# One expert of a mixture-of-experts stage on quarters instead of halves of TensorE's columns, with its gather moved ahead of a branch

## Chip, cores and metric

One core of a Trainium2 chip runs the whole kernel in one launch. The metric is device time in microseconds (us) of that core, smaller is better. Engines are called as the profile calls them: PE (matrix multiply), PEld (its weight loads), DVE (vector), ACT (scalar), POOL (GpSimd) and SP (the queue that issues the large transfers). A `q` behind a name (PEldq, SPq) is the engine's sequencer, which runs branches, register loads and DMA issues.

## What is computed

Two layers of a diffusion backbone on 256 latent and 256 context tokens of width 1024. Each layer mixes tokens (attention and a gated convolution) and then channels. The first layer's channel mixer is dense; the second layer's is the part that matters here:

```
def moe_swiglu(h, w_router, w_gu, w_down):          # h: 256 x 1024
    logits = (h @ w_router).astype(jnp.float32)     # 8 experts
    top_v, top_i = lax.top_k(logits, TOP_K)         # TOP_K = 2
    top_w = jax.nn.softmax(top_v, axis=-1)
    gates = jnp.sum(jax.nn.one_hot(top_i, 8) * top_w[..., None], axis=-2)
    for e in range(8):
        g, u = jnp.split(h @ w_gu[e], 2, axis=-1)   # w_gu[e]: 1024 x 7168
        y = y + gates[..., e:e + 1] * ((silu(g) * u) @ w_down[e])   # w_down[e]: 3584 x 1024
```

Everything is float32, and each expert's weights are 42 pieces of 1 MB (28 of `w_gu`, 14 of `w_down`), read once from HBM.

## The kernel before

**Ranks.** After routing, experts are sorted by their token counts on the chip. Place 0 holds expert 0, places 1 to 7 the others, from the fullest to the emptiest. The heavy places are `HS = (0, 2, 3, 1)` and the light ones `LS = (4, 5, 6, 7)`, both in the order in which they are worked on. `keyi[p]` is eight times the count of place p plus its expert's number.

**Arms.** `tc.If(odd > 0)` holds a general path (`any_experts`) for counts that fit no plan. Its Else arm runs the plan of pairs: `plans[0]` (places 0, 2, 3 beside 4, 5 and most of 6), and then, under `tc.If(k1 > 8 * 128 + 7)`, `plans[1]` (place 1 beside the rest of 6 and all of 7) in one of two arms. `few` is the arm in which place 1 has more than 128 tokens, up to 160: its first 128 tokens run like those of every heavy expert, its last ones (at most 32) as a second small block.

**A heavy operation** (`Hg` gate, `Hu` up, `Hd` down) uses two pieces of 1 MB. Each piece is split by ACT and DVE into a high and a low part in reduced-precision format (L99, L100), and PE makes three products of them (`mm3`, L537 to L539) for 128 tokens. In the arm `few` it is followed by the last tokens' products, straight from the unsplit piece in float32, with 32 tokens on each quarter of PE's 128 columns, so four slices of the weights at a time (L1711 for gate and up, L1781 for down).

**A light operation** (`Lg`, `Lu`, `Ld`) also uses two pieces, unsplit, in float32, with 64 tokens on each half of PE's columns, so two slices of the weights at a time (L1735 gate and up, L1801 down). `Ht` and `Lt` turn the activations (L1745, L1756).

**Order.** `schedule` interleaves them: while heavy chunk s is at its gate and up, light chunk s - 1 is too, and the down products of the chunks before follow. A chunk is 1024 hidden columns, the last one 512. `plans[1]` has 48 operations that take weights, 96 pieces in all; 14 of them are `Lg` or `Lu` of place 7 and 7 are `Ld` of place 7. Inside `run_pairs` each of PE, DVE and ACT keeps the order of the program. Small jobs (gathers of an expert's tokens, `combine` of its output) stand in a queue `bg` and advance by one step after an operation; what is left is done at the end of `run_pairs`.

**Pieces.** `Mixed` issues the transfers in order on SP's queue into eight buffers (`RAW_N`). In the arm `few` a piece keeps its buffer until the last tokens' products have read it.

**The gather of the last tokens**, `few_tokens`, stands at the head of `plans[1]`: two steps on DVE build the selection (L1668, L1669), eight matmuls gather the rows (L1674), six transposes place them (L1679, L1682).

**The end.** `finish` adds the last expert's output, normalises and stores.

Of the kernel before, what the change touches and what calls it, by code (L numbers as in the profile page):

```python
# [8 lines left out]
F32 = mybir.dt.float32  # L9
# [158 lines left out]
def kernel(ctx: ExitStack, tc: tile.TileContext, x, c, cx, c_ctx, w_ada, b_ada, norm_g,  # L168
# [18 lines left out]
    def tiny(shape, name="s", dt=F32):  # L187
        return sm.tile(shape, dt, name=name, tag="sm")
# [1427 lines left out]

    X32, SL32 = {}, {}

    def light_gather(p):

        n = LS.index(p)
        tl_ = ring.tile([128, 512], F32R, "x2", 2 + n % 2)
        sl = tl_[:, 0:256].rearrange("p (t n) -> p t n", t=2)
        SL32[p] = tl_[:, 256:512]
        x32 = ring.tile([128, 512], F32, "x32", n % 2)
        X32[p] = x32.rearrange("p (k n) -> p k n", k=KD)
        for t in range(2):
            V.tensor_scalar(sl[:, t, :].rearrange("p (g n) -> p g n", g=2),
                            iota[:, 0:64].unsqueeze(1).to_broadcast([128, 2, 64]), posms[:, t, p:p + 1], None,
                            op0=OP.is_equal)  # L1630
        yield from pause(3)
        for h in range(2):
            pb, q = tbank(), slice(64 * h, 64 * h + 64)
            for i, (t, src) in enumerate(((0, hth), (0, htl), (1, hth), (1, htl))):
                PE.matmul(pb, sl[:, t, :], src[:, t, hsl(h)], start=i == 0, stop=i == 3)
            A.copy(x2f[q, :], pb[q, :])
            yield
        pb = tbank()
        for t in range(2):
            PE.transpose(pb[:, 128 * t:128 * t + 128], sl[:, t, :].bitcast(F32), ident)  # L1640
        A.copy(SL32[p], pb[:, :256])
        yield
        pb = tbank()
        for c in range(4):
            PE.transpose(pb[:, 128 * c:128 * c + 128], x2f[:, 128 * c:128 * c + 128], ident)
        A.copy(x32.rearrange("p (h c n) -> p c h n", h=2, c=4), pb.rearrange("p (c h n) -> p c h n", c=4, h=2))
        yield

    def run_pairs(plan, few, todo):

        arm[0] = "few pair" if few else "pair"
        Wb.keep = few
# [8 lines left out]
        x2, t2 = x2f[:, 0:256].rearrange("p (k n) -> p k n", k=KD), x2f[:, 256:512]  # L1661
        st2 = x2r[:, 256:512]

        def few_tokens(p):
            sl2 = x2r[:, 0:256].rearrange("p (t n) -> p t n", t=2)
            for t in range(2):
                p2 = tiny([128, 1], "p2")
                V.tensor_scalar(p2, posms[:, t, p:p + 1], -128.0, None, op0=OP.add)  # L1668
                V.tensor_scalar(sl2[:, t, :].rearrange("p (g n) -> p g n", g=4),  # L1669
                                iota[:, 0:32].unsqueeze(1).to_broadcast([128, 4, 32]), p2, None, op0=OP.is_equal)  # L1670
            for h in range(2):
                pb, q = hb[h], slice(32 * h, 32 * h + 32)
                for i, (t, src) in enumerate(((0, hth), (0, htl), (1, hth), (1, htl))):
                    PE.matmul(pb, sl2[:, t, :], src[:, t, hsl(h)], start=i == 0, stop=i == 3)  # L1674
                A.copy(fact[q, :], pb[q, :])
            yield
            pb = tr0[:, 0:256]
            for c in range(4):
                PE.transpose(pb[:, 64 * c:64 * c + 64], fact[0:64, 128 * c:128 * c + 128], ident[0:64, 0:64])  # L1679
            A.copy(x2.rearrange("p (h c) n -> p c h n", h=2), pb.rearrange("p (c h n) -> p c h n", c=4, h=2))  # L1680
            for t in range(2):
                PE.transpose(facc[:, 128 * t:128 * t + 128], sl2[:, t, :].bitcast(F32), ident)  # L1682
            A.copy(st2, facc[:, :256])
            yield

        def heavy_gu(p, c, i, up):
            x1, n = XG[p], CHUNKS[c][1]
            nb, w4, per = n // 512, n // 4, 2048 // n
            tokens = few_tokens(p) if few and c == i == 0 and not up else None
            if tokens:  # L1690
                next(tokens)
            Wb.floor = Wb.gi if few else None
            raws = []
            for t in range(2 * i, 2 * i + 2):
                wh, wl = Wb.get("mg")
                raws.append(Wb.last_raw)
                for k in range(per):
                    kk = per * t + k
                    for b in range(nb):
                        q = slice(512 * b, 512 * b + 512)  # L1700
                        mm3(hb[b], x1[:, 0, kk, :], x1[:, 1, kk, :], wh[:, k, q], wl[:, k, q], kk == 0, kk == KD - 1)
            if tokens:
                next(tokens)
            o2 = tr0[:, 256 * up:256 * up + w4]
            if few:

                for t in range(2 * i, 2 * i + 2):
                    for k in range(per):
                        kk = per * t + k
                        for g_ in range(4):  # L1710
                            PE.matmul(o2[32 * g_:32 * g_ + 32, :], x2[:, kk, :],  # L1711
                                      raws[t % 2][:, k, w4 * g_:w4 * g_ + w4], start=kk == 0, stop=kk == KD - 1)
            Wb.floor = None
            if i == nb - 1:
                evac(nb, hact, hb, up)
                if few:
                    evac(1, [fact[:, 0:w4]], [o2], up)

        def evac(nb, act, o, up):
            for b in range(nb):  # L1720
                if up:
                    V.tensor_tensor(act[b], act[b], o[b], op=OP.mult)
                else:
                    A.activation(act[b], o[b], AF.Silu)

        def light_gu(p, c, i, up):
            n = CHUNKS[c][1]
            w2, per = n // 2, 2048 // n
            o = lb[:, 0:w2]
            for t in range(2 * i, 2 * i + 2):  # L1730
                raw = Wb.get("lg")
                for k in range(per):
                    kk = per * t + k
                    for g_ in range(2):
                        PE.matmul(o[64 * g_:64 * g_ + 64, :], X32[p][:, kk, :], raw[:, k, w2 * g_:w2 * g_ + w2],  # L1735
                                  start=kk == 0, stop=kk == KD - 1)
            if i == n // 512 - 1:
                evac(1, [lact[:, 0:w2]], [o], up)

        def heavy_turn(p, c, i):  # L1740
            n = CHUNKS[c][1]
# [9 lines left out]
                A.copy(t2[:, 0:n // 4], tr0[:, 0:n // 4])  # L1751

        def light_turn(p, c, i):
            w2 = CHUNKS[c][1] // 2
            for j in range(w2 // 128):
                PE.transpose(lb[:, 128 * j:128 * j + 128], lact[:, 128 * j:128 * j + 128], ident)  # L1756
            A.copy(lt[:, 0:w2], lb[:, 0:w2])  # L1757

        def heavy_down(p, c, i):
            nb = CHUNKS[c][1] // 512  # L1760
# [30 lines left out]
                bg.append(combine(gates[:, :, p], parts, wait=1 if p == 1 else 2))  # L1791

        def light_down(p, c, i):
            nj = CHUNKS[c][1] // 256
            final = c == len(CHUNKS) - 1
            for t in range(2):
                raw = Wb.get("ld")
                for f in range(2):
                    g_, j = divmod(4 * i + 2 * t + f, nj)
                    for h in range(2):  # L1800
                        PE.matmul(lacc[64 * h:64 * h + 64, :], lt[:, 128 * j + 64 * g_:128 * j + 64 * g_ + 64],  # L1801
                                  raw[:, f, hsl(h)], start=c == 0 and i == t == f == 0, stop=final and t == 1 and f == 1)
            if final:
                o = [ring.tile([128, 512], F32R, "x2", i) for i in range(2)]
                split_hl(*o, lacc)
                S_["parts"] = [(SL32[p], in_halves(o))]
                if p != LS[-1]:
                    bg.append(combine(gates[:, :, p], S_["parts"], wait=2))

# [62 lines left out]
    for t in range(2):  # L1872
        V.scalar_tensor_tensor(gate[:, t, :], gate[:, t, :], e2[:, t:t + 1], sel[:, t, :], op0=OP.mult, op1=OP.mult)
    by_rank(gates, gate)
    odd = nc.values_load(bad[0:1, 0:1], min_val=0, max_val=NE)
    k1 = nc.values_load(keyi[0:1, 1:2], min_val=0, max_val=8 * S + 7)
    ids = [0] + [nc.values_load(eid[0:1, p:p + 1], engines=[mybir.EngineType.SP], min_val=0, max_val=NE - 1)
                 for p in range(1, NE)]
    back0 = again()
    with tc.If(odd > 0) as odd_arm:  # L1880

        Wm = Stream(nc, ring, moe_items(range(NE)))
        Wm.lag, Wm.ahead, Wm.sahead = lambda: first(-LAG["experts"]), RAW_N, SPL_N - 1
        any_experts()
# [3 lines left out]
    with odd_arm.Else():  # L1888
        run_pairs(plans[0], False, {
            ("Hg", 0, 0, 0): [lambda: light_gather(4)], ("Hg", 0, 1, 0): [lambda: gather([2, 3], posms, True)],  # L1890
            ("Hg", 0, 3, 0): [lambda: light_gather(5)], ("Hg", 2, 1, 0): [lambda: gather([1], posms, True)],
            ("Hg", 2, 3, 0): [lambda: light_gather(6)], ("Hg", 3, 2, 0): [lambda: light_gather(7)]})
        back1 = again()
        Wb.hold = len(Wb.items)
        with tc.If(k1 > 8 * 128 + 7) as few_arm:  # L1895
            finish(gates[:, :, LS[-1]], run_pairs(plans[1], True, {}))
        back1()
        with few_arm.Else():
            finish(gates[:, :, LS[-1]], run_pairs(plans[1], False, {}))
# [47 lines left out]
```

## Time and profile before

| | us |
|---|---|
| median of 3 runs | 1918.11 |
| lowest, highest | 1916.24, 1918.60 |
| profiled execution | 1916.19 |
| its span, first to last instruction | 1914.4 |
| PE busy over the span | 1818.3 |
| DVE busy, ACT busy | 948.4, 812.2 |
| bytes moved | 521.12 MB, mean 272 GB/s |

The profiled execution's time is its span and 1.8 us around it; it lies 1.9 us under the median. The stage with the experts runs from about 976 us to the end of the span. Busy PE time includes modelled ends of pipelined matmuls, so the pace of a matmul is read from the distance of two starts.

### The profile page before, as it was taken

The page shows a single profiled execution, that of the slowest core. Times are in us where ns is not written, and L with a number is a line of the kernel's source. Part 1 is how long each engine was busy: PE and PEld are TensorE (multiplying, and loading weights), DVE is VectorE, ACT ScalarE, POOL GpSimd, SP SyncE. Part 2 cuts the span into 40 slices and gives each one's busy share as a digit, 9 for nine tenths or more (in the row PEclk, how much of TensorE's full clock was granted, in tenths as well). Part 3 has the DMA queues.
Part 4 walks back from the last instruction along what each step waited for, and adds up shares of the span by engine and source line. Part 5 has one row for each costly group of instructions (what it writes and reads, how often), then busy time and mean ns, then how long its engine had stood idle before and what let it go on. Part 6 is the DMA issues. An engine that isn't in the chain of part 4 may idle for free. (4 is left out here: it accounts for less than half of the span.)

```text
span 1914.4 us, 23955 instructions
## 1 busy us (share of the span) xinstructions
PE 1818.3 (95%) x9321; PEld 1273.7 (67%) x9321; DVE 948.4 (50%) x1310; ACT 812.2 (42%) x1194; POOL 79.0 (4%) x139
## 2 busy tenths in 40 slices
PE   6999999999999999999779999999999996999997
PEld 3866679877777888877666656566565653655553
DVE  3344578322232748536556545665455543545433
ACT  3354457221212547438445535454354443434322
POOL 2200110000000000200200000000000000000001
PEclk9999999999999999999969999999999998999999
DMA  9956286645552656733438999999999998898994
GB/s 337 200 174 203 105 287 209 208 154 176 172 179 89 220 180 235 174 104 111 176 107 339 368 404 404 409 409 406 406 404 409 410 404 349 323 375 334 373 376 187
DMA packets 223760, 521.12 MB, mean 272 GB/s; under 512 B 30040, under 2 KB 83856, under 8 KB 223632
## 3 DMA queue, kind: packets, MB, share of 16 engines
q1 hardware_dynamic: 223152, 519.27, 74.3%
q8 instruction: 77, 1.26, 0.3%
q14 instruction: 51, 0.42, 0.1%
q10 hardware_dynamic: 480, 0.18, 0.0%
HBM read 518.31 MB, written 3.13 MB: 272 GB/s over the span
## 5 line engine op out<-in xcount | busy, mean ns | idle before, releaser
L100 DVE TENSOR_TENSOR wlor<-rawr,whir 128x1024 fp32r<-128x1024 f32 x336 | 395.7, 1221 | 386.3 <-ACT whir L99 375.0
L99 ACT CAST whir<-rawr 128x1024 fp32r<-128x1024 f32 x336 | 335.4, 1049 | 340.9 <-DMA rawr<-in_w_gu_moe_dram 163.1
L100 DVE TENSOR_TENSOR wlo<-raw,whi 128x1024 fp32r<-128x1024 f32 x188 | 224.6, 1222 | 113.6 <-ACT whi L99 74.5
L99 ACT CAST whi<-raw 128x1024 fp32r<-128x1024 f32 x192 | 193.0, 1049 | 143.8 <-PE pg L538 40.3
L1735 PE MATMUL gur<-rawr,x32r 128*64 128x512 f32 (+1 forms) x1024 | 205.1, 547 | 6.5 <-ACT lar L1757 5.3
L537 PE MATMUL gur<-whir,xgr 128*128 128x512 f32 x448 | 181.0, 404 | 11.8 <-issue 6.7
L538 PE MATMUL gur<-wlor,xgr 128*128 128x512 f32 x448 | 176.0, 393 | 0.0
L539 PE MATMUL gur<-whir,xgr 128*128 128x512 f32 x448 | 175.6, 392 | 0.0
L1735 PEld LDWEIGHTS gur<-rawr,x32r 128*64 128x64 f32 x1024 | 69.5, 137 | 118.2 <-issue 100.0
L537 PEld LDWEIGHTS gur<-whir,xgr 128*128 128x128 f32 x448 | 84.9, 190 | 51.1 <-issue 22.0
L1801 PE MATMUL pd<-rawr,lar 128*64 128x512 f32 x448 | 101.7, 598 | 0.5 <-ACT lar L1757 0.5
L539 PEld LDWEIGHTS gur<-whir,xgr 128*128 128x128 f32 x448 | 84.8, 189 | 18.4
L538 PEld LDWEIGHTS gur<-wlor,xgr 128*128 128x128 f32 x448 | 84.9, 189 | 16.0
L537 PE MATMUL pg<-hh,whi 128*128 128x512 f32 (+1 forms) x256 | 95.0, 372 | 0.0
L539 PE MATMUL pu<-hh,wlo 128*128 128x512 f32 (+1 forms) x256 | 93.0, 363 | 0.4 <-DVE wlo L100 0.4
L539 PE MATMUL pg<-hh,wlo 128*128 128x512 f32 (+1 forms) x256 | 93.1, 364 | 0.0
L537 PE MATMUL pu<-hh,whi 128*128 128x512 f32 (+1 forms) x256 | 92.9, 363 | 0.0
L538 PE MATMUL pg<-hl,whi 128*128 128x512 f32 (+1 forms) x256 | 92.9, 363 | 0.0
L538 PE MATMUL pu<-hl,whi 128*128 128x512 f32 (+1 forms) x256 | 92.8, 362 | 0.0
L945 DVE TENSOR_TENSOR act<-sg,pu 128x512 f32<-128x512 f32 (+1 forms) x32 | 19.8, 620 | 147.1 <-PE pu L539 128.7
L537 PE MATMUL py<-whi,ah 128*128 128x512 f32 x224 | 87.4, 390 | 0.0
L539 PE MATMUL py<-whi,al 128*128 128x512 f32 x224 | 86.8, 390 | 0.6 <-DVE al L550 0.6
(391 smaller groups left out, 2972.5 us busy)
## 6 DMA issues: line engine op xcount, KB each, us to landing
rawr<-in_w_gu_moe_dram SPq DMA_DIRECT2D x224, 1024.0 KB
rawr<-in_w_down_moe_dram SPq DMA_DIRECT2D x112, 1024.0 KB
raw<-in_w_ada_dram SPq DMA_DIRECT2D x48, 1024.0 KB
raw<-in_w_gu_dense_dram SPq DMA_DIRECT2D x32, 1024.0 KB
raw<-in_w_down_dense_dram SPq DMA_DIRECT2D x28, 1024.0 KB
raw<-in_w_in_dram SPq DMA_DIRECT2D x24, 1024.0 KB
raw<-in_w_out_dram SPq DMA_DIRECT2D x12, 1024.0 KB
BM<-rep SPq DMA_DIRECT2D x8, 512.0 KB
```

Source lines behind the costliest of these rows:

```text
L99: nc.scalar.copy(hi[:, q], flat[:, q])
L100: (nc.gpsimd if g == "G" else nc.vector).tensor_tensor(lo[:, q], flat[:, q], hi[:, q].bitcast(F32), op=OP.subtract)
L537: PE.matmul(o, wh, mh, start=first, stop=False, skip_group_check=shared)
L538: PE.matmul(o, wh, ml, start=False, stop=False, skip_group_check=shared)
L539: PE.matmul(o, wl, mh, start=False, stop=last, skip_group_check=shared)
L945: V.tensor_tensor(act[f // 4][:, f % 4, s0:s0 + n], sg, pu, op=OP.mult)
L1735: PE.matmul(o[64 * g_:64 * g_ + 64, :], X32[p][:, kk, :], raw[:, k, w2 * g_:w2 * g_ + w2], start=kk == 0, stop=kk == KD - 1)
L1801: PE.matmul(lacc[64 * h:64 * h + 64, :], lt[:, 128 * j + 64 * g_:128 * j + 64 * g_ + 64], raw[:, f, hsl(h)], start=c == 0 and i == t == f ...
```

## The change

Place 7 may run on quarters. A new condition inside the arm `few`, `tc.If(k7 < 8 * 33)`, is true if it has at most 32 tokens; then `groups(7)` is 4, and its products take 32 tokens on each quarter of PE's columns, like the last tokens' products of the heavy expert. The Else arm keeps halves. `quarter_slots` builds the selection for the way back; it and `few_gather` (the former `few_tokens`) are queued in `bg` during `plans[0]`, behind `light_gather(7)`. One more value is loaded into registers (`k7`), and the outer `If` names its false arm as the one that is to follow next in the code.

```diff
+    def quarter_slots(p):
+        sl = LQ.rearrange("p (t n) -> p t n", t=2)
+        for t in range(2):
+            V.tensor_scalar(sl[:, t, :].rearrange("p (g n) -> p g n", g=4),
+                            iota[:, 0:32].unsqueeze(1).to_broadcast([128, 4, 32]), posms[:, t, p:p + 1], None,
+                            op0=OP.is_equal)
+        yield from pause(2)
+        pb = tbank()
+        for t in range(2):
+            PE.transpose(pb[:, 128 * t:128 * t + 128], sl[:, t, :].bitcast(F32), ident)
+        A.copy(LQ, pb[:, :256])
+        yield
...
+    def few_gather(p):
...
+        yield from pause(2)
+        for h in range(2):
+            pb, q = tbank(), slice(32 * h, 32 * h + 32)
+            for i, (t, src) in enumerate(((0, hth), (0, htl), (1, hth), (1, htl))):
+                PE.matmul(pb, sl2[:, t, :], src[:, t, hsl(h)], start=i == 0, stop=i == 3)
+            A.copy(fact[q, :], pb[q, :])
+            yield
...
-            tokens = few_tokens(p) if few and c == i == 0 and not up else None
-            if tokens:
-                next(tokens)
...
+        def groups(p):
+
+            return 4 if quarters and p == LS[-1] else 2
...
-                    for g_ in range(2):
-                        PE.matmul(o[64 * g_:64 * g_ + 64, :], X32[p][:, kk, :], raw[:, k, w2 * g_:w2 * g_ + w2],
+                    for g_ in range(G):
+                        PE.matmul(o[m * g_:m * g_ + m, :], X32[p][:, kk, 0:m], raw[:, k, wg * g_:wg * g_ + wg],
                                   start=kk == 0, stop=kk == KD - 1)
...
-            w2 = CHUNKS[c][1] // 2
-            for j in range(w2 // 128):
+            wg = CHUNKS[c][1] // groups(p)
+            for j in range(wg // 128):
...
+                        q = 64 * h + 32 * f if G == 4 else 64 * h
+                        PE.matmul(lacc[q:q + m, :], lt[:, 128 * j + m * g_:128 * j + m * g_ + m], raw[:, f, hsl(h)],
...
+    k7 = nc.values_load(keyi[0:1, 7:8], min_val=0, max_val=8 * S + 7)
...
-    with tc.If(odd > 0) as odd_arm:
+    with tc.If(odd > 0, preferred_fallthrough_block=False) as odd_arm:
...
-            ("Hg", 2, 3, 0): [lambda: light_gather(6)], ("Hg", 3, 2, 0): [lambda: light_gather(7)]})
+            ("Hg", 2, 3, 0): [lambda: light_gather(6)], ("Hg", 3, 2, 0): [lambda: light_gather(7), lambda: quarter_slots(7), lambda: few_gather(1)]})
...
-            finish(gates[:, :, LS[-1]], run_pairs(plans[1], True, {}))
+            with tc.If(k7 < 8 * 33) as quarter_arm:
+                finish(gates[:, :, LS[-1]], run_pairs(plans[1], True, {}, True))
+            back1()
+            with quarter_arm.Else():
+                finish(gates[:, :, LS[-1]], run_pairs(plans[1], True, {}))
```

## Rows read from the trace of the kernel before

**Rows 1.** Windows of two stretches: busy us of each engine, PE clock, DMA share, GB/s

```profile
1100.00:1590.00 490.00, 474.88 (x2176) 292.28 (x2174) 258.92 (x258) 221.05 (x262) 0.00 (x0) 0.99 1.03 406
1640.00:1880.00 240.00, 237.48 (x1519) 138.82 (x1518) 112.31 (x112) 92.58 (x111) 0.00 (x0) 1.00 0.95 368
```

**Rows 2.** Waits of SP's queue, 1500 us to the end: total, times, longest

```profile
SPq L80 <- PE tr L1711: 112.9, 26, 22.3
```

**Rows 3.** Timeline of PE: start, us, line, operation, count [idle before]

```profile
1682.15 1.93 PE L1711 MATMUL tr<-rawr,x2f 128*32 128x256 f32 x32
1684.02 3.65 PE L1735 MATMUL gur<-rawr,x32r 128*64 128x512 f32 x16
1687.60 0.50 PE L537 MATMUL gur<-whir,xgr 128*128 128x512 f32 x1
...
1693.27 1.93 PE L1711 MATMUL tr<-rawr,x2f 128*32 128x256 f32 x32
...
1726.61 1.92 PE L1781 MATMUL pd<-rawr,x2f 128*32 128x512 f32 x16
1728.46 0.73 PE L1363 MATMUL tr<-oer,str 128*128 128x512 f32 x2
1729.12 3.65 PE L1801 MATMUL pd<-rawr,lar 128*64 128x512 f32 x16
1732.71 0.74 PE L1363 MATMUL tr<-oer,str 128*128 128x512 f32 x2
```

**Rows 4.** Windows behind the first and the second branch, columns as in Rows 1

```profile
983.00:990.00 7.00, 7.00 (x21) 5.47 (x20) 2.21 (x2) 2.37 (x3) 0.00 (x0) 0.60 0.01 4
...
1620.00:1624.00 4.00, 3.91 (x10) 3.18 (x11) 0.38 (x3) 0.78 (x2) 0.00 (x0) 0.56 0.27 109
1624.00:1630.00 6.00, 6.00 (x29) 4.39 (x28) 0.00 (x0) 0.45 (x2) 0.00 (x0) 1.00 0.00 0
```

**Rows 5.** Timeline of all engines around the second branch

```profile
1605.69 1.99 ACT L99 CAST whir<-rawr 128x1024 fp32r<-128x1024 f32 x2 [5.91 <-DMA rawr<-in_w_gu_moe_dram]
...
1607.20 0.66 PE L1756 MATMUL gur<-kc,sgr 128*128 128x128 f32 x4
...
1616.21 1.99 ACT L99 CAST whir<-rawr 128x1024 fp32r<-128x1024 f32 x2 [5.51 <-DMA rawr<-in_w_gu_moe_dram]
...
1619.57 0.15 DVE L1668 TENSOR_SCALAR p<-posms 128x1 f32<-128x1 f32 x1
...
1620.09 0.80 PE L1674 MATMUL gur<-hth,x2r 128*128 128x512 f32 x1 [12.24 <-DVE p L1668]
...
1623.60 0.40 PE L537 MATMUL gur<-whir,xgr 128*128 128x512 f32 x1
...
1629.43 0.46 PE L1679 MATMUL tr<-kc,sgr 64*128 64x64 f32 x4
...
1630.35 1.93 PE L1711 MATMUL tr<-rawr,x2f 128*32 128x256 f32 x32
```

**Rows 6.** Lines with branches, at three places: duration ns, start us

```profile
L1880 PEldq COMPARE_BRANCH  x1: 6329/6329/6329, 976.0 to 976.0; - x1
...
L1895 PEldq COMPARE_BRANCH  x1: 82/82/82, 1603.6 to 1603.6; - x1
...
L1895 PEldq COMPARE_BRANCH  x1: 3678/3678/3678, 1901.6 to 1901.6; - x1
```

**Rows 7.** PE at the first branch, and the load of one register there

```profile
982.42 0.79 PE L537 MATMUL gur<-whir,xgr 128*128 128x512 f32 x1 [6.71 <-issue]
...
L1876 PEldq TENSOR_LOAD <-keyi x1: 312/312/312, 975.6 to 975.6; - x1
```

**Rows 8.** The end of `plans[1]` on PE, and POOL's last store wait

```profile
1894.90 3.65 PE L1801 MATMUL pd<-rawr,lar 128*64 128x512 f32 x16 [0.46 <-ACT lar L1757]
1898.48 0.73 PE L1363 MATMUL tr<-oer,str 128*128 128x512 f32 x2
...
1912.50 0.09 POOL L1309 MEMSET actr<- 1x1 f32 x1 [0.63 <-DMA out_dram<-actr]
```

More of the change, by code (lines that the diff above doesn't have):

```diff
@@ L1617 @@
     X32, SL32 = {}, {}
+    LQ = ring.tile([128, 512], F32R, "x2", 3)[:, 0:256]
+    def quarter_slots(p):
[10 more added lines that the diff above has]
+        yield
     def light_gather(p):
@@ L1647, in light_gather, with run_pairs @@
         yield
-    def run_pairs(plan, few, todo):
+    def few_gather(p):
+        sl2 = x2r[:, 0:256].rearrange("p (t n) -> p t n", t=2)
+        fact = ring.tile([128, 512], F32, "sg", 1)
+        for t in range(2):
+            p2 = tiny([128, 1], "p2")
+            V.tensor_scalar(p2, posms[:, t, p:p + 1], -128.0, None, op0=OP.add)
+            V.tensor_scalar(sl2[:, t, :].rearrange("p (g n) -> p g n", g=4),
+                            iota[:, 0:32].unsqueeze(1).to_broadcast([128, 4, 32]), p2, None, op0=OP.is_equal)
+        yield from pause(2)
[5 more added lines that the diff above has]
+            yield
+        pb = tbank()
+        for t in range(2):
+            PE.transpose(pb[:, 128 * t:128 * t + 128], sl2[:, t, :].bitcast(F32), ident)
+        A.copy(x2r[:, 256:512], pb[:, :256])
+        yield
+        pb = tbank()[:, 0:256]
+        for c in range(4):
+            PE.transpose(pb[:, 64 * c:64 * c + 64], fact[0:64, 128 * c:128 * c + 128], ident[0:64, 0:64])
+        A.copy(x2f[:, 0:256].rearrange("p (h c n) -> p c h n", h=2, c=4), pb.rearrange("p (c h n) -> p c h n", c=4, h=2))
+        yield
+    def run_pairs(plan, few, todo, quarters=False):
         arm[0] = "few pair" if few else "pair"
@@ L1662, in run_pairs @@
         st2 = x2r[:, 256:512]
[L1664 to L1684, printed above, removed]
         def heavy_gu(p, c, i, up):
@@ L1701, in heavy_gu @@
                         mm3(hb[b], x1[:, 0, kk, :], x1[:, 1, kk, :], wh[:, k, q], wl[:, k, q], kk == 0, kk == KD - 1)
-            if tokens:
-                next(tokens)
             o2 = tr0[:, 256 * up:256 * up + w4]
@@ L1724, in evac @@
                     A.activation(act[b], o[b], AF.Silu)
+        def groups(p):
+            return 4 if quarters and p == LS[-1] else 2
         def light_gu(p, c, i, up):
-            n = CHUNKS[c][1]
-            w2, per = n // 2, 2048 // n
-            o = lb[:, 0:w2]
+            n, G = CHUNKS[c][1], groups(p)
+            wg, per, m = n // G, 2048 // n, 128 // G
+            o = lb[:, 0:wg]
             for t in range(2 * i, 2 * i + 2):
@@ L1733, in light_gu @@
                     kk = per * t + k
-                    for g_ in range(2):
-                        PE.matmul(o[64 * g_:64 * g_ + 64, :], X32[p][:, kk, :], raw[:, k, w2 * g_:w2 * g_ + w2],
+                    for g_ in range(G):
+                        PE.matmul(o[m * g_:m * g_ + m, :], X32[p][:, kk, 0:m], raw[:, k, wg * g_:wg * g_ + wg],
                                   start=kk == 0, stop=kk == KD - 1)
             if i == n // 512 - 1:
-                evac(1, [lact[:, 0:w2]], [o], up)
+                evac(1, [lact[:, 0:wg]], [o], up)
         def heavy_turn(p, c, i):
@@ L1753, in light_turn @@
         def light_turn(p, c, i):
-            w2 = CHUNKS[c][1] // 2
-            for j in range(w2 // 128):
+            wg = CHUNKS[c][1] // groups(p)
+            for j in range(wg // 128):
                 PE.transpose(lb[:, 128 * j:128 * j + 128], lact[:, 128 * j:128 * j + 128], ident)
-            A.copy(lt[:, 0:w2], lb[:, 0:w2])
+            A.copy(lt[:, 0:wg], lb[:, 0:wg])
         def heavy_down(p, c, i):
@@ L1793, in light_down @@
         def light_down(p, c, i):
-            nj = CHUNKS[c][1] // 256
+            G = groups(p)
+            nj, m = CHUNKS[c][1] // 128 // G, 128 // G
             final = c == len(CHUNKS) - 1
@@ L1800, in light_down @@
                     for h in range(2):
-                        PE.matmul(lacc[64 * h:64 * h + 64, :], lt[:, 128 * j + 64 * g_:128 * j + 64 * g_ + 64],
-                                  raw[:, f, hsl(h)], start=c == 0 and i == t == f == 0, stop=final and t == 1 and f == 1)
+                        q = 64 * h + 32 * f if G == 4 else 64 * h
+                        PE.matmul(lacc[q:q + m, :], lt[:, 128 * j + m * g_:128 * j + m * g_ + m], raw[:, f, hsl(h)],
+                                  start=c == 0 and i == t == 0 and (f == 0 or G == 4),
+                                  stop=final and t == 1 and (f == 1 or G == 4))
             if final:
@@ L1805, in light_down @@
                 split_hl(*o, lacc)
-                S_["parts"] = [(SL32[p], in_halves(o))]
+                S_["parts"] = [(LQ if G == 4 else SL32[p], in_halves(o))]
                 if p != LS[-1]:
```

## The prediction

> **What bounds the kernel now.** I read the windows of the expert stage first, then the waits, then the timeline, because PE is near full everywhere and the share over the span tells nothing. The stage has two regimes [rows 1]. In the 490 us from 1100 the transfers run at 406 GB/s with their engines full: they set the pace, and PE keeps its fast clock (0.99) though it waits for them now and then. In the 240 us from 1640, which belong to `plans[1]`, they run at 368 GB/s, and SP's longest waits are for the last tokens' products (112.9 us in 26 waits) to give a buffer back [rows 2]. There PE sets the pace. One period (two heavy pieces, two light ones) shows it [rows 3]: 1682.15 to 1693.27, 11.12 us without a gap: last tokens 1.87, light 3.58, heavy 5.67.
>
> Between the regimes lies a hole. PE ends `plans[0]` at 1607.9 and starts `plans[1]`'s first weight product at 1623.60 [rows 5]. The reader should follow it backwards: the first gather matmul (1620.09) waited 12.24 us for DVE's selection (1619.57), and DVE, which keeps its program order, stood behind the split of the fifth piece, which ACT could begin only when it landed, at 1616.21. The pieces that PE needs first were there since 1605.69. Meanwhile the eight buffers fill, and the transfers stop: 109 GB/s from 1620, 0 from 1624 to 1630 [rows 4].
>
> Two lesser places. At the first branch PE's compare-and-branch takes 6.33 us, at the second 0.08 [rows 6]: the first jumps to its Else arm, the second falls into the arm behind it. PE's gap there is 6.71 us, with nothing awaited [rows 7]. And the run ends 15.9 us after the last light down product (1898.48 to 1914.4), in a chain of combine, norm and store [rows 8].
>
> **The change, part by part.**
>
> *Condition.* The reference's router, worked with its default inputs, gives 65, 71, 138, 45, 96, 43, 26 and 28 tokens to the experts. Place 1 has 138, place 7 has 26: the quarter arm is entered. Place 6 has 28 and stays on halves.
>
> *First branch.* Its false arm now follows it in the code. If it then costs what the second costs, PE starts 6.33 - 0.08 = 6.25 us earlier; the register load that is added (0.31 us on PE [rows 7]) goes off. Behind the branch the buffers are full, and transfers rest (4 GB/s from 983 to 990 [rows 4]) until PE frees them; so they start earlier by as much, and the gain is carried on. Bounds: +0.3 (the jump stays) to -6.3; I take -5.9, since the two branches are the same instruction and differ only in jumping.
>
> *Moved gather, and the new block.* Now in `bg` during `plans[0]`: eight matmuls at 0.24 us (5.67 over 24 [rows 3]), eight transposes at most at 0.23 (0.92 for six with their wait [rows 5] is less), so at most 3.8 us of PE, and some small operations on DVE and ACT, which are busy for half of the span at most. From `Hg 3 2 0` to the end of `plans[0]` 22 operations advance the queue; four steps of the combine before, seven of place 7's gather and nine new ones make 20, so nothing should be left for the end. The cover is the transfers: in that regime four pieces need 10.3 us (1.0486 MB at 406 GB/s is 2.58 us each), and PE for heavy and light 5.67 + 3.58 = 9.25. Five such periods give 5 us. I take 0; without the cover it is 3.8.
>
> *The hole.* PE need no longer wait for the fifth piece. It can start on the first piece when `plans[0]` ends, 1607.9; the low half of the second piece is ready some 4 us after it. I take 1610 (bounds 1608 to 1612), against 1623.60: 13.6 us of PE, and the transfers never stop.
>
> *Quarters.* The form exists in the trace: the last tokens' products are the same shape over the same pieces. Gate and up cost 3.58 on halves, 1.87 on quarters; down 3.59 (1729.12 to 1732.71) and 1.85 (1726.61 to 1728.46) [rows 3]. Fourteen operations by 1.71 and seven by 1.74 are 36.1 us of PE. ACT and DVE read half the width of place 7's results; neither is the bound, so 0.
>
> *Where the bound goes.* The gain of PE can't be taken whole, since a period would be 9.4 us of PE and 10.3 of transfers. So I walk both. PE: 1898.5 - 1623.6 = 274.9, less 36.1, less the transposes that went (0.9), is 237.9; from 1610 it ends at 1848. Transfers: the first piece is in at 1605.7, 95 more at 2.58 end at 1851.1, and half a quarter operation (0.9) follows: 1852. They aren't in step, however. The first 40 pieces are heavy on PE (ten heavy operations with last tokens at 7.54, one without at 5.67, five lights of place 6 at 3.58, four of place 7 at 1.87, some 5 us of turns and combines: 111 us, to 1721), while their transfers end at 1706. Eight buffers are 20.7 us of transfer, of which an operation holds 7.5, so a lag of 13 is free and PE's 15 costs a few us of stopped transfers. The other 56 pieces need 120 us of PE and 145 of transfers: there the transfers bind to the end. Cost of the lag 0 to 8, I take 5. The last product ends at 1857 instead of 1898.5: -41.5 (bounds -46.5 and -38.5).
>
> Here a page of the Trainium skill speaks against the change. "DMA: Bandwidth & Descriptors", section "Bandwidth", puts what HBM gives one core at about 358 GB/s and says that this binds for loads from HBM, though it lists 425 for one core with its neighbour idle. By the first figure a piece takes 2.93 us, the last would land at 1884, and this part would be about -14 instead of -41.5. The 406 GB/s over 490 us of this trace contradict it [rows 1].
>
> *Tail.* The chain behind the last product is unchanged. But PE leaves three arms instead of one: it paid 3.68 us at 1901.6 for one jump [rows 6], so three are 11 to 19 us, to 1913 to 1921, where the run waits for the stores until 1912.5 [rows 8]. 0 to +8; I take +1, as the ends may be one jump.
>
> *Sum.* -5.9 - 41.5 + 1 = -46.4 from the profiled execution's 1916.2 is 1869.8; the median of before lies 1.9 above it, so 1872. Ends: all gains and no lag 1864; half the branch, full lag and full tail 1883.
>
> **The rivals.**
>
> *Transfers hardly go faster in this arm (0.10).* Here pieces are held longer than in `plans[0]`, and 368 GB/s may be what eight buffers allow. For it: no long stretch of `plans[1]` ran faster. Against: SP waits for PE, not the reverse [rows 2]. At 368 a piece takes 2.85 us, 95 end at 1876.4, and the last product at 1877.3: -21.2 - 5.9 + 1, so 1892.
>
> *The order of the code does not help (0.08).* The first branch still jumps, or the inner one jumps in its stead, or the tail pays. Against: the second branch, built like the inner one, fell through. 1878 to 1886.
>
> *The quarter arm is not entered (0.03).* If the count is over 32 on the chip, the hole and the branch are gained, but PE still binds: -13.6 - 0.9 - 5.9 + 1, so 1899. Against: 26 is far from 32.
>
> *Slower: the clock falls (0.04).* PE would now wait in most periods, and a pause of 12 us took its clock to half: at 1620 to 1624 it was granted 0.56 [rows 4], and a gather matmul took 0.43 us (1620.09 to 1623.60 for eight) instead of 0.24. At 1.2 GHz a period is twice 9.4, 18.8 us, 8.5 more than the transfers. The 46 us are gone when 6 of about 22 periods run so; if all did, the kernel would be at 2060. Against: the waits would be 0.9 us each, and where waits like that occur now (1100 to 1590) the clock was 0.99 [rows 1].
>
> **How the numbers follow.** My forecast has 0.72, the four rivals 0.25, the rest 0.03 goes to unforeseen costs, half of them slower. The time is the forecast's, 1872. The range runs from its lower end, 1864, through its upper end, 1883, to the first rival's 1892: it takes in 0.72, 0.08 and most of 0.10. What a measurement tells from no change is about 0.2%, 3.8 us. Faster: 0.72 + 0.10 + 0.08 + 0.03 and a little of the rest, 0.94. Slower: the clock and half the rest, 0.05. Same: 0.01.
>
> **What would show it.** The branch: PE's compare-and-branch near 976 under 0.2 us. The hole: first heavy product of `plans[1]` within 5 us of the last of `plans[0]`, no window of 4 us without transfers. Quarters: place 7's products in 32 columns, 1.9 us an operation. The bound: periods of place 7 near 10.3 us, 400 GB/s or more in the last 130 us, ACT and PE waiting for pieces, PE's clock still near 1. The tail: 16 us from the last down product to the end. I am wrong if transfers stay under 385 GB/s while PE waits, if the clock drops in that stretch, or if the end waits for PE's jumps.

## The result, and the profile after

| | before | after |
|---|---|---|
| median, us | 1918.36 | 1888.78 (1887.64 to 1889.71) |
| profiled execution, its span | 1916.19, 1914.4 | 1887.64, 1885.8 |
| mean granted PE clock | 0.978 | 0.977 |

After over before is 0.9847 [0.983, 0.9864]: 29.6 us less, where 46.4 were forecast. A second measurement of the same kernel gave 1887.49. Every part came, and none of the rivals holds as it was put; the sum is short by 17 us.

**The parts that came.** First the branches, as lines with durations in ns and start times, of the kernel after:

```profile
L1905 PEldq COMPARE_BRANCH  x1: 98/98/98, 976.0 to 976.0; - x1
...
L1920 PEldq COMPARE_BRANCH  x1: 68/68/68, 1605.3 to 1605.3; - x1
L1921 PEldq COMPARE_BRANCH  x2: 68/1765/3462, 1605.4 to 1872.7; - x2
```

The 6.33-us jump [rows 6] is gone, and no other took its place: both inner branches fall through. At the end one jump of 3.46 us is left, as before (3.68). The price is PE's alone: at the first branch of the kernel before, ACT, DVE, POOL and SP took the same jump in 0.05 to 0.07 us. The timeline of PE after, at the places of [rows 3, 5, 7 and 8]:

```profile
976.14 0.79 PE L537 MATMUL gur<-whir,xgr 128*128 128x512 f32 x1 [1.22 <-issue]
...
1581.04 0.79 PE L1678 MATMUL pd<-hth,x2r 128*128 128x512 f32 x1 [5.87 <-DVE p L1671]
...
1608.83 0.66 PE L1776 MATMUL gur<-kc,sgr 128*128 128x128 f32 x4
...
1614.91 1.93 PE L1727 MATMUL tr<-rawr,x2f 128*32 128x256 f32 x32
...
1676.23 1.93 PE L1727 MATMUL tr<-rawr,x2f 128*32 128x256 f32 x32
1677.98 1.91 PE L1755 MATMUL gur<-rawr,x32r 128*32 128x256 f32 x32
...
1685.48 1.93 PE L1727 MATMUL tr<-rawr,x2f 128*32 128x256 f32 x32
...
1867.81 1.92 PE L1824 MATMUL pd<-rawr,lar 128*32 128x512 f32 x16 [0.41 <-ACT lar L1777]
1869.66 0.73 PE L1363 MATMUL tr<-oer,str 128*128 128x512 f32 x2
```

PE starts the stage at 976.14 instead of 982.42. The hole behind the second branch [rows 5] is closed: the last turn of `plans[0]` starts at 1608.83, the first weight product of `plans[1]` at 1609.25, and at 1614.91, a heavy operation later, the last tokens' products run, which ran at 1630.35 before. Place 7 works on 32 columns at 1.9 us an operation, and where PE sets the pace a period is 9.25 us (1676.23 to 1685.48) instead of 11.12. The tail is 16.1 us (1869.66 to the end of the span), 15.9 before.

**Where the rest stayed.** Windows after (columns as in [rows 1]):

```profile
983.00:990.00 7.00, 7.00 (x32) 5.79 (x32) 5.01 (x6) 4.78 (x6) 0.00 (x0) 1.00 0.87 306
1100.00:1590.00 490.00, 471.51 (x2142) 289.03 (x2141) 257.90 (x261) 222.68 (x265) 0.00 (x0) 0.98 1.03 405
...
1560.00:1600.00 40.00, 34.13 (x142) 17.40 (x139) 17.51 (x20) 17.05 (x21) 0.00 (x0) 0.91 0.99 384
...
1610.00:1870.00 260.00, 242.95 (x1955) 156.04 (x1954) 120.99 (x123) 99.36 (x124) 0.00 (x0) 0.95 0.95 367
...
1680.00:1720.00 40.00, 38.14 (x264) 24.96 (x264) 22.27 (x23) 15.65 (x18) 0.00 (x0) 0.96 1.02 408
...
1760.00:1800.00 40.00, 36.84 (x304) 22.64 (x296) 21.65 (x24) 16.50 (x21) 0.00 (x0) 0.91 0.98 376
1800.00:1840.00 40.00, 33.35 (x257) 21.52 (x253) 12.78 (x14) 8.37 (x9) 0.00 (x0) 0.87 1.02 400
```

Over `plans[1]` as a whole (1610 to 1870) the transfers move 367 GB/s. That is more than the 342 of before between the same places (1607.20 to 1894.90, with the hole in it), but no more than the 368 of before behind the hole [rows 1]. PE is idle for 17 of 260 us with its clock at 0.95. Neither is full. Single stretches do reach 400 to 408 GB/s.

Between the start of a kernel's last turn in `plans[0]` and that of its last light down product lies `plans[1]`; before it, from the first weight product on, lies `plans[0]`. Split so, the two misses separate (us, from one profiled execution each; the forecast's figure for `plans[1]` runs from the turn's start at 1607.2 to its end of the last product, 1857, less the 1.85 us of that product):

| stage | before | forecast | after |
|---|---|---|---|
| `plans[0]` | 624.8 | 624.8 | 632.7 |
| `plans[1]` | 287.7 | 247.9 | 259.0 |

So 7.9 us were lost in `plans[0]` and 11.1 in `plans[1]`. The branch's extra 0.4 and the 1 us that the tail did not take leave 17.6 of the 17.8 by which the profiled execution missed 1869.8.

### The profile page after: what moved, and what is told of

It is laid out like the page before. It is cut to its first block, busy times and chain, and to the rows that moved or that the text cites. A ratio compares the mean times of both kernels' runs of the same rounds, so it can differ in the third digit from the quotient of the medians.

```text
span 1885.8 us, 24473 instructions
## 1 busy us (share of the span) xinstructions
PE 1790.2 (95%) x9572; PEld 1271.3 (67%) x9572; DVE 946.3 (50%) x1312; ACT 812.3 (43%) x1195; POOL 79.0 (4%) x139
## 5 line engine op out<-in xcount | busy, mean ns | idle before, releaser
L1755 PE MATMUL gur<-rawr,x32r 128*64 128x512 f32 (+3 forms) x1280 | 184.5, 479 | 8.0 <-ACT lar L1777 4.3
L537 PE MATMUL gur<-whir,xgr 128*128 128x512 f32 x448 | 181.2, 404 | 5.7 <-DVE tlr L1767 4.4
L538 PE MATMUL gur<-wlor,xgr 128*128 128x512 f32 x448 | 175.9, 393 | 0.0
L1755 PEld LDWEIGHTS gur<-rawr,x32r 128*64 128x64 f32 (+1 forms) x1280 | 69.2, 130 | 101.5 <-issue 76.5
L537 PEld LDWEIGHTS gur<-whir,xgr 128*128 128x128 f32 x448 | 84.8, 189 | 41.5 <-issue 12.7
L538 PEld LDWEIGHTS gur<-wlor,xgr 128*128 128x128 f32 x448 | 85.0, 190 | 15.9
L537 PE MATMUL pg<-hh,whi 128*128 128x512 f32 (+1 forms) x256 | 95.0, 372 | 0.0
L537 PE MATMUL pu<-hh,whi 128*128 128x512 f32 (+1 forms) x256 | 92.9, 363 | 0.0
L538 PE MATMUL pg<-hl,whi 128*128 128x512 f32 (+1 forms) x256 | 92.9, 363 | 0.0
L538 PE MATMUL pu<-hl,whi 128*128 128x512 f32 (+1 forms) x256 | 92.8, 362 | 0.0
L1824 PE MATMUL pd<-rawr,lar 128*64 128x512 f32 (+1 forms) x448 | 92.1, 614 | 0.4 <-ACT lar L1777 0.4
L537 PE MATMUL py<-whi,ah 128*128 128x512 f32 x224 | 87.4, 390 | 0.0
```

The costliest lines, as they stand in the source:

```text
L537: PE.matmul(o, wh, mh, start=first, stop=False, skip_group_check=shared)
L538: PE.matmul(o, wh, ml, start=False, stop=False, skip_group_check=shared)
L1755: PE.matmul(o[m * g_:m * g_ + m, :], X32[p][:, kk, 0:m], raw[:, k, wg * g_:wg * g_ + wg], start=kk == 0, stop=kk == KD - 1)
L1824: PE.matmul(lacc[q:q + m, :], lt[:, 128 * j + m * g_:128 * j + m * g_ + m], raw[:, f, hsl(h)], start=c == 0 and i == t == 0 and (f == 0 or ...
```

## The experiments

The theory after the result: (a) PE's saving in `plans[1]` is real but turns into pauses, because ACT and DVE keep the order of the program, and small jobs on which PE waits stand behind splits of pieces that have not landed; a pause also halves PE's clock for some us. Against it: (b) PE's own work still binds; (c) buffers that are held for the last tokens' products bind the transfers. All ratios are to the kernel before.

**The three parts alone.** The first takes the kernel before and one line of the diff:

```diff
-    with tc.If(odd > 0) as odd_arm:
+    with tc.If(odd > 0, preferred_fallthrough_block=False) as odd_arm:
```

> The kernel before with only the outer branch's false arm placed next. Own step: PE's compare-and-branch at 976 falls from 6.33 us to about 0.1, the arm starts 6.2 us earlier and all behind it shifts: 1912. Rival: the gain is swallowed where transfers or the hole before the last plan set the pace, or is paid back by a jump at the end: 1916 to 1918.

Measured: 1911.04 (before 1918.13), 0.9968 [0.9959, 0.9977]: -7.1 us. Its branch, and PE behind it:

```profile
L1880 PEldq COMPARE_BRANCH  x1: 98/98/98, 975.5 to 975.5; - x1
...
975.65 0.79 PE L537 MATMUL gur<-whir,xgr 128*128 128x512 f32 x1 [0.47 <-issue]
```

The lead is kept to the end: `plans[0]` takes 624.1 and `plans[1]` 288.1 us. The second takes the kernel before and moves the gather only:

```diff
-            tokens = few_tokens(p) if few and c == i == 0 and not up else None
...
-            ("Hg", 3, 2, 0): [lambda: light_gather(7)]})
+            ("Hg", 3, 2, 0): [lambda: light_gather(7), lambda: few_gather(1)]})
```

> The kernel before with only the last tokens' gather moved into the queue of the plan before (no quarters, the outer branch as before). Own step: the hole of 13.6 us goes, PE binds afterwards: 1904. Order theory (a selection on DVE stands behind the split of a piece that has not landed, now inside the plan before): part of it comes back as a pause of PE of some 6 us and a slow clock there: 1907 to 1912. If the pause there costs as much as the hole: 1918.

Measured: 1905.13, 0.9934 [0.9913, 0.9956]: -13.0 us. It is a difference of two larger numbers: `plans[0]` grew by 6.0 us to 630.8, `plans[1]` shrank by 17.1 to 270.6. PE's longest wait from 1560 on lies inside `plans[0]`, at the moved gather (total, times, longest):

```profile
PE pd L1672 <- ACT sgr L1663: 4.8, 1, 4.8
```

The third takes quarters without the other two: the kernel after, with `few_gather` taken out of `bg`, the old `few_tokens` back at the head of `plans[1]`, and the branch as it was.

> The changed kernel with the gather back at the head of the last plan and the outer branch as before: quarters alone. Own step: PE loses 36 us of work after the hole, transfers stood still for 9 us, so both walks end near 1861 instead of 1898: 1882. Order theory: PE pauses behind DVE and ACT and its clock falls, as in the changed kernel, so some 15 us of it are lost: 1897 to 1903. If quarters gave nothing: 1918.

Measured: 1903.21, 0.9938 [0.9918, 0.9959]: -14.9 us, where 36.1 us of PE's work went. `plans[1]` takes 272.5. Behind the hole PE's waits come to 19 us, for the same operations as in the kernel after; before they were 3. Together the three alone give 35.0 us, the whole change 29.6: they overlap rather than help each other.

**Is PE's work still the bound (b)?** In the kernel after, place 7's products are cut to 32 columns of weights each:

```diff
-                        PE.matmul(o[m * g_:m * g_ + m, :], X32[p][:, kk, 0:m], raw[:, k, wg * g_:wg * g_ + wg],
+                        w_ = 32 if G == 4 else wg
+                        PE.matmul(o[m * g_:m * g_ + m, 0:w_], X32[p][:, kk, 0:m], raw[:, k, wg * g_:wg * g_ + w_],
...
```

> The changed kernel with place 7's products on 32 of each slice's columns only (the rest of its outputs is left out), so that its light operations cost PE half or less. If PE's work still binds there: about 1 us less for each of 21 operations, 1868 to 1872. If transfers and the order of DVE and ACT bind: under 8 us less, 1881 to 1889, and PE only waits longer.

Measured: 1885.2 (before 1918.13), 0.9845 [0.9823, 0.9867], so 3.6 us under the kernel after by the medians and nothing by the ratios. In `plans[1]` PE is busy for 218.6 us instead of 241.9, but the stage takes 252.8 us instead of 259.0. PE's waits grow as its work shrinks, in the list of its waits from 1560 to 1872:

```profile
PE pd L1678 <- DVE p L1671: 7.7, 1, 7.7
PE tr L1363 <- DVE y L1365: 6.9, 3, 5.0
PE gur L1756 <- ACT sgr L1740: 6.6, 1, 6.6
PE pdn0r L537 <- ACT whir L99: 5.9, 3, 3.3
```

(b) falls: 23 us of PE's work are worth 6 in its stage, and the longest waits are for the same operations as in the kernel after.

**Do held buffers bind (c)?** In the kernel after, both pieces of a heavy operation are first read by the last tokens' products and then by the three heavy ones, so that what those products hold is given back earlier:

```diff
             for t in range(2 * i, 2 * i + 2):
                 wh, wl = Wb.get("mg")
                 raws.append(Wb.last_raw)
+                if quarters:
+                    halves_.append((t, wh, wl))
+                else:
+                    main(t, wh, wl)
...
+            for a in halves_:
+                main(*a)
```

> The changed kernel with the last tokens' gate and up products ahead of the heavy products of the same pieces, so that each piece's buffer comes free some 5.6 us earlier. Buffer theory (transfers thin because eight buffers are held too long): up to the 17 us that my forecast missed, 1872 to 1880. Order theory: the waits for DVE and ACT stay, 1884 to 1890.

Measured: 1886.71 (before 1917.82), 0.9837 [0.9815, 0.9858], 2 us under after, which the intervals can't tell from nothing. By itself this frees nothing that counts. The opposite was meant to follow, transfers six pieces ahead instead of eight in the quarter arm:

```diff
             with tc.If(k7 < 8 * 33) as quarter_arm:
+                Wb.ahead = RAW_N - 2
...
```

> The changed kernel with transfers only six pieces ahead in the quarter arm instead of eight. Buffer theory: two pieces are 5.2 us of lead, and with every stop of PE transfers stop too: 1900 or more. Order theory: PE's pauses are set by landings and order, six pieces are still more than an operation needs: under 6 us more, to 1895.

Measured: 1885.16, 0.9824 [0.9805, 0.9843]. This run tells nothing of (c): the ring still has eight buffers and PE's instructions keep their order; all that the edit did was to place a few splits on ACT and DVE behind small jobs instead of ahead of them. That the time did not rise, and `plans[1]` came down to 252.0 us, fits (a).

**The order on ACT and DVE (a).** In `run_pairs` the splits of the pieces ahead (`Wb.ready`) are written before the next step of the small jobs. This run turns the two round after a down product, in the quarter arm alone, and asks for no splits between two light operations:

```diff
-            if after[0][1:] != "t":
+            if quarters and op[1] == "d":
+                bg_step(1)
+            if after[0][1:] != "t" and not (quarters and op[0] == after[0][:1] == "L"):
                 Wb.ready(3 if op[0] == "L" else 2)
...
-            if op[1] == "d" or op[1] != "t" and not few:
+            if not quarters and op[1] == "d" or op[1] != "t" and not few:
```

> The changed kernel with another order of small jobs in the quarter arm: combine steps are issued ahead of the next pieces' splits instead of behind them, and no splits are issued between two light operations. Order theory: PE's waits for DVE's adds (8.5 us) and for ACT's silu (3.7 us) and the slow spells behind them go: 1874 to 1882. Buffer theory: PE only waits for pieces instead, 1885 to 1890.

Measured: 1879.19 (before 1917.82), 0.9809 [0.979, 0.9827]: 9.6 us under after by the medians, 7.3 by the ratios to the kernel before (0.9847 and 0.9809). Nothing of PE's work, the buffers or the transfers was changed. `plans[0]` is as long as in the kernel after (632.9); `plans[1]` takes 248.7 us instead of 259.0, within 1 us of the forecast's 247.9. PE's waits after, from 1609.5 to 1870:

```profile
PE tr L1363 <- DVE y L1365: 5.1, 2, 3.3
PE gur L1755 <- ACT sgr L1740: 3.7, 1, 3.7
PE tr L1770 <- DVE y L1365: 3.2, 1, 3.2
PE pdn0r L537 <- ACT whir L99: 2.6, 1, 2.6
```

and in the reordered kernel, from 1560 to 1872:

```profile
PE pd L1678 <- DVE p L1671: 6.0, 1, 6.0
PE pdn0r L537 <- ACT whir L99: 4.5, 2, 2.5
PE tr L1770 <- DVE y L1365: 3.0, 1, 3.0
...
PE tr L1363 <- DVE y L1365: 0.6, 1, 0.6
PE gur L1755 <- ACT sgr L1740: 0.4, 1, 0.4
```

The waits for a combine (L1365) in front of L1363 and for a silu (L1740) are nearly gone; the wait at L1770 stayed, and so did the one at the moved gather (L1678), which the edit does not reach. Waits for splits (L537 and L538) grew, from 3.4 to 6.5 us. In all PE's idle time in `plans[1]` fell from 17.1 to 12.0 us, which is half of the stage's gain. The other half is busy time: the same 1946 matmuls kept PE busy for 241.9 us in the kernel after, at a granted clock of 0.95, and for 236.7 here, at 0.98. The window of 1610 to 1860, columns as in [rows 1], of the kernel after:

```profile
1610.00:1860.00 250.00, 233.36 (x1893) 153.05 (x1895) 118.37 (x120) 98.39 (x121) 0.00 (x0) 0.95 0.97 375
```

and of the reordered one, with more PE work done in it, a faster clock and more bytes:

```profile
1610.00:1860.00 250.00, 237.97 (x1957) 151.98 (x1955) 120.76 (x123) 99.58 (x124) 0.00 (x0) 0.98 0.99 382
```

**The pause at the moved gather.** The selection of the last tokens is built earlier, in the first step of `quarter_slots`, and the two pauses of `few_gather` go, which also moves its matmuls two steps forward:

```diff
     def quarter_slots(p):
+        few_select(1)
...
     def few_gather(p):
-        for t in range(2):
-            p2 = tiny([128, 1], "p2")
...
-        yield from pause(2)
```

> The changed kernel with the selection for the last tokens' gather built earlier on DVE, with the selection for place 7, three steps ahead of its matmuls. Order theory: PE's pause of 5.9 us before the gather and the slow clock behind it go, the last plan starts up to 9 us earlier: 1880 to 1885. If transfers set the end whatever PE does: less than 3 us, 1886 to 1889.

Measured: 1881.99 (before 1917.82), 0.9819 [0.9802, 0.9835]: 6.8 us under after by the medians, 5.4 by the ratios, whose intervals overlap. The stage shows it better: `plans[0]` takes 628.2 us instead of 632.7, and over all kernels with the moved gather 632.2 to 634.6 us where quarters are built and the old selection is kept (six of them), 627.8 to 630.4 where it is built earlier (four). The longest wait there is now for ACT, and the transfers are back at 405 GB/s (last line, a window with columns as in [rows 1]):

```profile
PE pd L1687 <- ACT sgr L1683: 2.2, 1, 2.2
...
1560.00:1600.00 40.00, 37.77 (x164) 20.99 (x162) 17.05 (x16) 16.95 (x22) 0.00 (x0) 0.96 1.03 405
```

**Both, and more.** The next three, measured beside the kernel after (1887.49, before 1916.83), put the edits together: the selection and the order; these and the early reading of the buffers; the selection and the order with place 7's products cut as above.

> The changed kernel with both changes of order: the earlier selection and the small jobs ahead of the splits. Order theory: the two remove pauses in different places, so their gains (6.8 and 9.6 us against 1888.8) add up: 1872. If both only gave the transfers back the same lead: 1878 to 1880.

> The kernel with both changes of order, and the last tokens' gate and up products ahead of the heavy ones, so that buffers come free some 5.6 us earlier. If, with the pauses gone, the eight buffers bind in the first half of the last plan: 4 to 10 us less than with both changes of order alone, 1862 to 1868. If not: within 3 us of it.

> The kernel with both changes of order, and place 7's products on 32 of each slice's columns only (the rest of its outputs is left out). It asks for the floor of the transfers in the last plan: by my forecast's walk they end near 1845, and the run near 1862 to 1866. If it stays within 4 us of the kernel with both changes of order, PE's work is no longer what keeps that one above the walk, and transfers or waits for them are.

Measured, with the two stages of one profiled execution each:

| kernel | median | ratio | `plans[0]` | `plans[1]` |
|---|---|---|---|---|
| after | 1887.49 | 0.985 [0.9828, 0.9873] | 632.8 | 257.8 |
| selection and order | 1879.31 | 0.9811 [0.9792, 0.983] | 630.4 | 250.3 |
| and early reading | 1871.22 | 0.9772 [0.975, 0.9794] | 627.8 | 246.6 |
| selection and order, cut | 1874.86 | 0.9783 [0.9763, 0.9804] | 629.9 | |

The first two gains did not add: 8.2 us instead of 16.4 (by the ratios 7.5 instead of 12.7), no more than the order alone. So the order theory's 1872 failed here, and 1879.31 lies where the rival had put it, on which both edits give the transfers the same lead back; no run tests that reading. Part of what is missing shows in `plans[0]`, where PE's wait for ACT came out at 4.9 us instead of 2.2:

```profile
PE pd L1687 <- ACT sgr L1683: 4.9, 1, 4.9
PE pdn0r L537 <- ACT whir L99: 4.6, 2, 2.4
```

The early reading, worth nothing that could be told alone, is worth 8.1 us on top of the two, and gives a kernel that beats both: 45.6 us under before. Of that, `plans[1]` shows 3.7 us; 2.6 lie in `plans[0]`, where the two kernels have the same code, so they are variation between executions. The 8.1 lie in the 4 to 10 us that the expectation gave if held buffers bind once the pauses are gone. The first 40 us of `plans[1]`, without the early reading and with it, speak for that:

```profile
1607.16:1647.16 40.00, 40.00 (x304) 28.17 (x303) 20.61 (x21) 18.11 (x21) 0.00 (x0) 1.00 0.94 359
...
1604.39:1644.39 40.00, 39.04 (x299) 27.42 (x298) 19.32 (x19) 18.37 (x21) 0.00 (x0) 1.00 1.01 390
```

Without it PE is busy throughout while the transfers move 359 GB/s; with it they move 390 there, and 394 instead of 385 over the whole of `plans[1]`. So (c) was refuted only for the kernel after, where the pauses came first. How much of the 3.7 is due to the buffers, and how much to PE having products at hand that need no split, is left open. In the cut kernel PE is busy for 17 us less in the first 230 us of the stage, and the run is 4.5 us shorter than with both edits alone, just outside the 4 us that the expectation had set as the limit: PE's work still counts, for about a quarter of itself. Its 1874.86 is above the 1862 to 1866 of the forecast's walk.

## Why the prediction was right, and where it failed

The forecast itself was 1872, its own upper end 1883. The measured 1888.78 lies in the stated range only because the range was stretched to the first rival's 1892, so that part was luck. Two of the prediction's three signs of being wrong appeared: the transfers stayed under 385 GB/s while PE waited (376 from 1760 to 1800), and PE's clock dropped in that stretch (0.91, then 0.87); the end did not wait for PE's jumps. Two slips of the sum matter little: both ends, 1864 and 1883, leave out the 1.9 us to the median that the forecast takes in (they would be 1865 and 1885), and PE's 111 and 120 us for the two parts of `plans[1]` add up to 231, where the walk has 238.

*Condition, first branch, tail: right.* The quarter arm ran. The jump went from 6.33 to 0.098 us, PE started 6.28 us earlier where 5.9 was taken, and the first part alone gave 7.1. The Trainium skill, "Runtime: NRT & Kernel Launch", section "Instruction fetch mechanics", says that a branch taken to a target outside the window of fetched code stalls the engine; the trace agrees in PE's time, 6.33 us taken and 0.10 fallen through, but shows nothing of a fetch, and the other engines took the same branch at no such price (0.05 to 0.07 us). The tail's +1 was 0: one jump, not three.

*The hole: right.* Moved alone, the gather took 17.1 us out of `plans[1]`: the 13.6 of the step, the 0.9 of the transposes, and 2.6 that it did not have.

*Moved gather, "I take 0; without the cover it is 3.8": failed.* It cost 6.0 us alone and 7.9 with the new block. The step counted PE's instructions (3.8) and named the transfers as their cover. What it left out is the wait: a selection made by DVE stands behind the split of the next piece, just as it did at the head of `plans[1]` [rows 5], only shorter. The timeline of ACT, DVE and PE after:

```profile
1577.16 1.99 ACT L99 CAST whir<-rawr 128x1024 fp32r<-128x1024 f32 x2 [9.99 <-DMA rawr<-in_w_down_moe_dram]
...
1578.24 2.36 DVE L100 TENSOR_TENSOR wlor<-rawr,whir 128x1024 fp32r<-128x1024 f32 x2 [10.40 <-ACT whir L99]
1580.51 0.15 DVE L1671 TENSOR_SCALAR p<-posms 128x1 f32<-128x1 f32 x1
```

DVE stood idle for 10.40 us, until ACT's half of the split came, and then made its own half first; the selection, 0.15 us long, came at 1580.51, and PE waited 5.87 us for it. Behind the pause PE's clock was granted 0.50 from 1580 to 1586, the gather matmuls came 0.43 us apart, and the transfers moved 384 GB/s in 1560 to 1600, where they moved 407 before. In the kernel with the gather alone it was a copy on ACT that PE waited for (4.8 us). The cover was there only for the work, not for the wait.

*Quarters: right in size.* 1.9 us an operation, period 9.25 where 9.4 was worked out.

*"Where the bound goes", cost of the lag "0 to 8, I take 5": failed.* The walk let PE and the transfers each run densely and charged one lag between them. PE's own walk went from 1610 to 1848. PE did start there (the branch's lead had gone in `plans[0]`), but it ended at 1870: 17 us are pauses, and it was busy for 243 us instead of 238, the stretches at half clock among the causes (with the order turned round the same work took 236.7). The kind of pause is seen on the timeline of the kernel after:

```profile
1824.37 0.73 PE L1363 MATMUL tr<-x2r,x2r 64*128 64x512 f32 x2
...
1826.03 1.99 ACT L99 CAST whir<-rawr 128x1024 fp32r<-128x1024 f32 x2 [0.56 <-DMA rawr<-in_w_down_moe_dram]
...
1827.16 2.35 DVE L100 TENSOR_TENSOR wlor<-rawr,whir 128x1024 fp32r<-128x1024 f32 x2
1829.43 0.75 DVE L1365 SCALAR_TENSOR_TENSOR y<-tr,gates,y 128x512 f32<-128x512 f32 x1
1830.23 1.22 PE L1363 MATMUL tr<-x2r,x2r 64*128 64x512 f32 x2 [3.28 <-DVE y L1365]
...
1831.97 0.63 PE L538 MATMUL pdn0r<-wlor,thr 128*128 128x512 f32 x1
1832.40 0.63 PE L539 MATMUL pdn0r<-whir,tlr 128*128 128x512 f32 x1
```

PE turns an output at 1824.37; the combine that empties the bank takes DVE 0.75 us. But it stands behind two splits, the second of a piece that ACT had to wait for, so it runs at 1829.43, and PE stands for 3.28 us. The products behind it then come 0.43 us apart instead of the 0.23 ahead of the pause. At 1850.12 it is ACT's turn: the silu at 1849.80 stands behind the split of 1847.90, and PE waits 3.74 us. Before, PE was late everywhere, so each split was done long before PE came to it, and the same order cost nothing: 3 us of waits from 1623 to 1899. The Trainium skill, "PSUM — Partial Sum Buffer", section "Engine vs sequencer instructions", says of ScalarE's and VectorE's queues that they are strictly first in, first out; the trace agrees, with combine and silu run behind the splits written before them, and PE's waits of 3.28 and 3.74 us. Reordering alone brought this stage to 248.7 us, and to 250.3 in the kernel with the earlier selection, against the forecast's 247.9. So the walk and its lag were about right in size, and the step that failed is that it let PE run without walking the order on ACT and DVE.

*The rivals.* "Transfers hardly go faster" has the right figure, 367 GB/s over `plans[1]`, mostly by another way: they stood because PE did, and the reordered kernel moves 382 in 1610 to 1860, where the kernel after moves 375. Its own way, eight buffers held too long, shows only where the pauses are gone: there the early reading brought 394 with the same eight buffers. The 358 GB/s of the Trainium skill, "DMA: Bandwidth & Descriptors", section "Bandwidth", are contradicted again, by 405 in 1100 to 1590 and 408 in 1680 to 1720; the 425 that the section lists for one core with its neighbour idle lie above both. "The clock falls" is true in a small measure: at most the 5.3 us of busy time that the reordered kernel got back in `plans[1]`. Windows after, stretches at and behind pauses:

```profile
1580.00:1586.00 6.00, 4.96 (x12) 2.17 (x14) 4.16 (x8) 1.72 (x2) 0.00 (x0) 0.50 0.93 373
...
1785.00:1791.00 6.00, 6.00 (x19) 3.29 (x12) 3.11 (x3) 1.46 (x3) 0.00 (x0) 0.50 1.03 406
...
1829.00:1836.00 7.00, 5.77 (x13) 4.16 (x14) 1.92 (x3) 0.00 (x0) 0.00 (x0) 0.51 1.05 389
```

Granted 0.50 is 1.2 GHz. The argument against it was the 0.99 of 1100 to 1590 [rows 1]. A mean of 0.99 over 490 us leaves room for some 10 us at half, and the step did not ask what one pause costs.

## What to carry to other kernels

When a change takes work off the engine that is late everywhere, walk the others in the order of their programs too: a short job behind a long one that waits for a transfer costs nothing while the first engine is late, and as much as the wait once it is on time. Price a moved step by what its first instruction stands behind at the new place, and not by its busy time alone. After such a change, look for the order that put the long-range work (here the splits ahead) in front of the small jobs: turning it round gave 7 to 10 us with no work removed. And try a refuted remedy again once the larger cause is gone: giving buffers back early was worth nothing that could be told before the order was turned round, and some 8 us in the kernel with both other edits.

## What was not expected of the hardware

PE's clock fell to half behind short pauses, in a stage where PE was otherwise near full: behind one of 3.28 us at 1830 (windows above), one of 2.61 us at 1814, and one of 1.86 us at 1712, as these windows after show:

```profile
1712.00:1717.00 5.00, 4.96 (x16) 3.95 (x17) 3.70 (x4) 2.26 (x3) 0.00 (x0) 0.66 1.03 410
...
1815.00:1819.00 4.00, 3.43 (x9) 2.71 (x10) 4.00 (x6) 2.20 (x3) 0.00 (x0) 0.57 1.03 410
```

The clock is 0.66 and 0.57 there. And the same code took 627.8 to 630.4 us in one stage of two kernels, with a wait of 2.3 us in one and 4.9 in the other: gains of under 3 us in a stage are not to be read from one execution each.
